# Layer 0's expert jobs packed anew: 42 jobs in place of 43, with the three unranked experts on nine lanes

## The chip, the cores and the metric

The kernel runs on one core of a Trainium2 chip. The metric is device time of one execution in microseconds (us). The core has a matmul engine (PE, with its weight loads as PEld), three engines for element work (DVE, ACT, POOL) and SP, which does no arithmetic: it issues transfers from device memory. POOL issues transfers too, above all those with a list of row numbers (indirect). Each engine takes its instructions in the order in which they stand, so an instruction that waits holds up all that stand behind it on that engine.

## The reference, cut to what matters

Two layers work on 256 latent and 256 context tokens of width 1024. Each layer has a mixer (attention) and then a mixture of experts; in layer 0 both kinds of token pass through the experts, 512 in all:

```python
def moe_ffn(h, w_router, e_bias, w_gate, w_up, w_down, s_gate, s_up, s_down):
    scores = jax.nn.sigmoid((h @ w_router).astype(jnp.float32))
    _, idx = lax.top_k(scores + e_bias.astype(jnp.float32), TOP_K)      # 8 of 64 experts
    wts = jnp.take_along_axis(scores, idx, axis=-1)
    wts = wts / wts.sum(-1, keepdims=True) * ROUTE_SCALE
    ...
    def expert_block(args):
        tok, e = args
        xb = h_pad[tok]
        a = jax.nn.silu(xb @ w_gate[e]) * (xb @ w_up[e])                # 1024 -> 256
        return a @ w_down[e]                                            # 256 -> 1024
    ...
    routed = jnp.zeros((n_tok + 1, d), h.dtype).at[slot_tok].add(y)[:n_tok]
    shared = (jax.nn.silu(h @ s_gate) * (h @ s_up)) @ s_down
    return routed + shared
```

All weights are 32-bit floats, so each of the 64 experts is 3 MB, and every expert is loaded once in each layer.

## The kernel before

**Jobs and lanes.** The experts' work is cut into jobs of 128 slots, one token in a slot. A job has four lanes of 32 slots, and an expert is given as many lanes as it is expected to need. The table is written out by hand in `Plan`: an entry `(column, lane, lanes, offset)` says that an expert's slots from `offset` on lie in these lanes of the job. An expert may be split over two jobs: the same column then stands in both, the second time with the offset at which the first ended. "Column" counts experts in the order in which jobs come to them.

**Unranked and ranked experts.** The first three experts (0, 1 and 2; `ahead` = `NS` = 3) are fixed, so that their weights can be loaded before the router's result is known (`static`). The other 61 are ordered by their number of tokens while the kernel runs (`ranks`); the expert at rank r has as many lanes as the table says, and its number is read from `ordi` before its weights are loaded. In layer 0 before the change, experts 0, 1 and 2 have four lanes each, that is jobs 0, 1 and 2.

**One job.** In the loop over `j`, a job's steps are: `experts` loads the weights of columns not loaded yet (SP; four half-megabyte pieces for gate and up, in two halves `h`, and one megabyte for down); `gate_up` multiplies the 128 slots by gate and up (PE; a job with more than one expert does it lane by lane, several lanes side by side); `act` on ACT and DVE; `gather` fetches the token rows for job j+2 (POOL, indirect; two buffers `xgs` in turn); `slots_T` transposes those of job j+1; `down`; and then the result. A job with one expert after the first three (`passes` 3) splits its weights into two parts and goes through `gate_up3` and `down3`.

**Where results go.** Jobs 3, 5, 7, ... 37 (`sent`) are added to a table in device memory by indirect transfers (`send`, POOL, one for each expert of the job). Every other job is placed by PE (`scatter`: 16 matmuls for a job, spread over the jobs that follow). Near the end `fetch(t)` reads the four token blocks of the two tables back on SP, and DVE adds them to `acc`. The first fetch must wait for the last send; each fetch stands in SP's order at the job in which it is called, behind that job's loads and ahead of the next job's.

**What sets the order.** PE and SP keep the order in which the code is written (`manual_schedule`); the order on DVE, ACT and POOL is a scheduler's. SP can run ahead of PE as far as buffers allow: weights lie in 11 buffers of 1 MB (`w8`), which is under four experts.

**Slots.** `slots` finds, for a group of jobs, which token is in which slot: `marks` on DVE, small matmuls on PE, then `idx`, the list that `gather` uses. The first group has `n0` jobs, those that need no ranking; the second has four, the others `SG` = 8.

Of the kernel before, what the change touches and what calls it, by code (L numbers as in the profile page):

```python
# [39 lines left out]
class Plan:  # L40
# [7 lines left out]
    def __init__(self, layer):  # L48
        self.rank, self.cap, self.jobs = [], [], []
        if layer == 0:  # L50
            self.ahead = 3
            by = {}
            d = self.ahead
            for lanes, n in ((5, 2), (4, 6), (3, 22), (2, 29), (1, 2)):
                by[lanes] = list(range(d, d + n))
                d += n
            for e in range(self.ahead):
                self.single(self.col(e, 4))
            for kind in "ptsptpstp5ptsptpstp5ptsptpstp":
                if kind == "5":  # L60
                    a, b = self.col(by[5].pop(0), 5), self.col(by[3].pop(0), 3)
                    self.single(a)
                    self.jobs.append([(a, 0, 1, 128), (b, 1, 3, 0)])
                elif kind == "s":
                    self.single(self.col(by[4].pop(0), 4))
                elif kind == "t":
                    a, b, c = self.col(by[3].pop(0), 3), self.col(by[3].pop(0), 3), self.col(by[2].pop(0), 2)
                    self.jobs.append([(a, 0, 3, 0), (b, 3, 1, 0)])
                    self.jobs.append([(b, 0, 2, 32), (c, 2, 2, 0)])
                elif by[1]:  # L70
                    self.pack((by[3].pop(0), 3), (by[1].pop(), 1))
                else:
                    self.pair(by[2].pop(0), by[2].pop(0))
        else:
            self.ahead = 4
            self.pair(0, 1)
            self.pair(2, 3)
            two, one = list(range(9, 41)), list(range(41, 64))
            big, three = [4, 5], [6, 7, 8]
            for kind in "ptptspt3ptpt3ptptspt3ptptp":  # L80
                if kind == "s":
                    self.single(self.col(big.pop(0), 4))
                elif kind == "3":
                    self.pack((three.pop(), 3), (one.pop(), 1))
                elif kind == "t":
                    self.pack((two.pop(0), 2), (one.pop(), 1), (one.pop(), 1))
                else:
                    self.pair(two.pop(0), two.pop(0))
        assert sorted(self.rank) == list(range(NE))
# [25 lines left out]
def tile_block(ctx: ExitStack, tc: tile.TileContext, I, out):  # L115
# [25 lines left out]
    def k4(shape, name="k4", dt=F32):  # L141
        return keep.tile(shape, dt, name=name, tag="k4", bufs=NK4)
# [226 lines left out]
    def modrow(l, nm, s):  # L369
        o = MODROW[nm] + (8 * s if nm in ("g1", "B2", "A2", "g2") else 0)  # L370
        return rows(rowsd[l, o:o + 8].rearrange("j p -> (j p)"), 128)
# [662 lines left out]
    def moe(l, out_of, nt, mp, pre=lambda: None, post=lambda: None):  # L1034
        n2 = nt * 128
        pl = PLANS[l]
        NS = pl.ahead
# [30 lines left out]
        def experts(cs):  # L1068
            new = [c for c in cs if c not in have]
            es = [ds(S.value_load(ordi[0:1, c:c + 1], min_val=0, max_val=NE - 1), 1) for c in new]  # L1070
            for c in new:
                have[c] = [[], None]
            for h in range(2):
                for c, e in zip(new, es):
                    have[c][0].extend(load_gu(e, (h,)))
            for c, e in zip(new, es):
                have[c][1] = early.pop(c, None) or expert_dn(c, e)
# [116 lines left out]
        jobs = pl.jobs  # L1194
        njob = len(jobs)
        wsl = mp.tile([128, njob], F32, name="wsl")
        tok = mp.tile([128, njob], F32, name="tok")
        idx = mp.tile([128, njob], I32, name="idx")
# [13 lines left out]
            else:  # L1212
                token_index(i_, t_, sl[:, :, 0])

        n0 = max(j for j in range(njob) if jobs[j][0][0] < NS) + 1
        group = [0, n0, n0 + 4] + list(range(n0 + 4 + SG, njob, SG)) + [njob]

        def all_slots():
# [172 lines left out]
        if l == 0:  # L1391
            xgs = [k4([128, D], f"xg{i}") for i in range(2)]
# [3 lines left out]
        def both(xs, j0, xT):  # L1396
            for k in range(2):
                xs[j0 + k] = lambda j, sl, k=k: xT[j // 4][:, j % 4, k * 128 + sl.start:k * 128 + sl.stop]
# [32 lines left out]
        def gather(x, idx_col):  # L1431
            G.indirect_dma_start(out=x, out_offset=None, in_=h2d[:n2, :],  # L1432
                                 in_offset=bass.IndirectOffsetOnAxis(ap=idx_col, axis=0),
                                 bounds_check=n2 - 1, oob_is_err=False)
# [210 lines left out]
        with tc.manual_schedule(engines={mybir.EngineType.SP, mybir.EngineType.PE}):  # L1645
# [45 lines left out]
            def slots_until(j):  # L1691
                while ready[0] < min(j, njob):
                    next(more)
# [51 lines left out]
            for j in range(njob - l):  # L1745
                segs = jobs[j]
                n_grp = 1 if sent and 2 < j < njob - 4 else GRP
                n_piece = -(-2 * nt // GRP)
                experts([sg_[0] for sg_ in segs])
                if j == njob - 1:  # L1750
                    g2s = [modrow(l, "g2", s) for s in range(nt // 2)]
                    for t in range(nt):
                        xt[t] = k4([128, D], f"xr{t}")
                        S.dma_start(xt[t], xd[t * 128:t * 128 + 128, :])
                ws = [have[sg_[0]] for sg_ in segs]
                if l and j % 2 == 0 and 0 < j < njob - 2:
                    gm = gather_mm(j + 2)
                    both(xs, j + 2, next(gm))
                xT = xs.pop(j)
                if l and j == njob - 2:  # L1760
                    next(gm, None)
                    g2s = [spread(raw[l][:, 5, 0])]
                if j == njob - 1:
                    for _ in sc:
                        pass
                    pre()
                p = pre_p.pop(j, None) or (gate_up3(xT, ws[0]) if passes[j] == 3 else gate_up(xT, ws, segs))
                if l and j == 0:
                    pre_p[1] = gate_up(xs[1], [have[sg_[0]] for sg_ in jobs[1]], jobs[1])
                a = act(p, wsl[:, j:j + 1])  # L1770
                if j == njob - 1:
                    root_table()
                    add[0] = fold(g2s)
                if l:
                    if j == 0:
                        next(rank)
                        sh_step(1)
                        slots_until(3)
                        gm = gather_mm(2)
                        both(xs, 2, next(gm))  # L1780
                        for _ in gm:
                            pass
                        experts((NS, NS + 1))
                        pre_p[2] = gate_up(xs[2], [have[sg_[0]] for sg_ in jobs[2]], jobs[2])
                        sh_step(1, 1)
                    next(gm, None)
                else:
                    if j + 2 < njob:
                        gather(xgs[j % 2], idx[:, j + 2:j + 3])
                    if j + 1 < njob:  # L1790
                        tr = slots_T(xgs[(j + 1) % 2], passes[j + 1])
                        xs[j + 1] = next(tr)
                        next(tr)
                for _ in range(n_piece // 2):
                    next(sc, None)
                aT = act_T(a, passes[j])
                if l == 0:
                    next(tr, None)
                if l == 0 and j == 0:
                    sh_step(3)  # L1800
                for _ in range(n_piece - n_piece // 2):
                    next(sc, None)
                ps = down3(aT, ws[0]) if passes[j] == 3 else down(aT, ws, segs)
                if j == 0:
                    for _ in rank:
                        pass
                next(more, None)
                next(more, None)
                slots_until(j + 1 + LA)
                if j >= n0 + 2:  # L1810
                    next(over, None)
                if l and j == njob - 2:
                    for _ in sc:
                        pass
                    add_x = add[0] = fold(g2s)
                if j in sent:
                    send(j, ps)
                else:
                    grp.append(place(ps, tok[:, j:j + 1]))
                if sent and 0 <= j - (njob - 5) < nt:  # L1820
                    fetch(j - (njob - 5))
                if len(grp) >= n_grp or j >= njob - 2:
                    for _ in sc:
                        pass
                    sc, grp = scatter(grp), []
# [169 lines left out]
```

## Time and profile before

| | us |
|---|---|
| median of three runs (1690.86 to 1693.26) | 1692.18 |
| the profiled execution | 1695.05 |
| its span, from first to last instruction | 1693.3 |
| PE busy in the span | 1572.6 (93%) |
| layer 0's experts, job 0's first matmul to the last job's | about 294 to 929 |

The profiled execution lies 2.9 us above the median, and 1.75 us of it lie outside the span. Times in the rows further down count from the span's start.

### The profile page before, as it was taken

The page shows a single profiled execution, that of the slowest core. Times are in us where ns is not written, and L with a number is a line of the kernel's source. Part 1 is how long each engine was busy: PE and PEld are TensorE (multiplying, and loading weights), DVE is VectorE, ACT ScalarE, POOL GpSimd, SP SyncE. Part 2 cuts the span into 40 slices and gives each one's busy share as a digit, 9 for nine tenths or more (in the row PEclk, how much of TensorE's full clock was granted, in tenths as well). Part 3 has the DMA queues.
Part 4 walks back from the last instruction along what each step waited for, and adds up shares of the span by engine and source line. Part 5 has one row for each costly group of instructions (what it writes and reads, how often), then busy time and mean ns, then how long its engine had stood idle before and what let it go on. Part 6 is the DMA issues. An engine that isn't in the chain of part 4 may idle for free. (4 is left out here: it accounts for less than half of the span.)

```text
span 1693.3 us, 27425 instructions
## 1 busy us (share of the span) xinstructions
PE 1572.6 (93%) x10238; PEld 928.5 (55%) x10238; DVE 784.8 (46%) x2118; ACT 452.0 (27%) x896; POOL 162.9 (10%) x148
## 2 busy tenths in 40 slices
PE   5999999999999999999979799999999998989984
PEld 3765687445445444444434577856656555555542
DVE  2465594356556544435256733347343422223225
ACT  2456311113223223223121333331221211112111
POOL 1003200012111121112200100011000000000001
PEclk9999999999999999999989899999999999999998
DMA  9948866779999999999979855256879999999992
GB/s 328 331 162 299 299 215 212 267 271 371 363 395 341 400 387 398 387 337 389 355 283 408 313 207 199 100 209 262 326 295 420 418 419 419 419 419 419 420 419 107
DMA packets 140808, 549.76 MB, mean 325 GB/s; under 512 B 14288, under 2 KB 23008, under 8 KB 109056
## 3 DMA queue, kind: packets, MB, share of 16 engines
q1 hardware_dynamic: 128368, 510.16, 77.0%
q0 software_dynamic: 12304, 37.81, 7.6%
q8 instruction: 82, 1.34, 0.3%
q14 instruction: 54, 0.44, 0.1%
HBM read 532.63 MB, written 21.05 MB: 327 GB/s over the span
## 5 line engine op out<-in xcount | busy, mean ns | idle before, releaser
L1331 PE MATMUL bank<-w,xT 128*32 128x512 f32 (+2 forms) x1488 | 254.0, 602 | 4.2 <-DMA w<-in_moe_w_up_dram 4.2
L1324 PE MATMUL bank<-w,xT 128*32 128x256 f32 (+2 forms) x2560 | 220.1, 395 | 29.1 <-DMA w<-in_moe_w_up_dram 25.4
L1342 PE MATMUL bank<-w,aT 128*32 128x512 f32 (+2 forms) x1232 | 234.6, 597 | 2.0 <-ACT aT L1298 2.0
L1279 DVE SCALAR_TENSOR_TENSOR a<-s,wsl,bank 128x256 f32<-128x256 f32 x71 | 34.1, 480 | 415.3 <-ACT s L1278 415.3
L1324 PEld LDWEIGHTS bank<-w,xT 128*32 128x32 f32 (+2 forms) x2560 | 130.9, 124 | 116.4 <-DMA w<-in_moe_w_up_dram 33.9
L1521 PE MATMUL bank<-yy,ss 128*128 128x512 f32 x624 | 177.6, 410 | 1.3 <-DVE yy L157 1.0
L1278 ACT ACTIVATE s<-bank 128x256 f32<-128x256 f32 x71 | 27.3, 385 | 544.2 <-PE bank L1331 278.7
L1513 DVE TENSOR_TENSOR acc<-acc,bank 128x512 f32<-128x512 f32 x228 | 149.5, 683 | 45.5 <-PE bank L1521 42.8
L1331 PEld LDWEIGHTS bank<-w,xT 128*32 128x32 f32 (+2 forms) x1488 | 78.6, 125 | 161.0 <-issue 155.0
L1342 PEld LDWEIGHTS bank<-w,aT 128*32 128x32 f32 (+2 forms) x1232 | 67.8, 124 | 120.0 <-issue 106.1
L1521 PEld LDWEIGHTS bank<-yy,ss 128*128 128x128 f32 x624 | 107.4, 190 | 22.5 <-DVE yy L157 2.7
L157 DVE TENSOR_TENSOR yy<-bank,yy 128x512 fp32r<-128x512 f32 x104 | 71.4, 688 | 89.8 <-ACT yy L157 89.8
L157 ACT CAST yy<-bank 128x512 fp32r<-128x512 f32 x104 | 60.9, 586 | 176.6 <-PE bank L1342 158.8
L1432 POOL DMA_INDIRECT xg<-h2d,idx x43 | 51.5, 1198 | 418.4 <-DVE acc L1513 216.8
L157 DVE TENSOR_TENSOR wl<-half,wh 128x1024 fp32r<-128x1024 f32 x35 | 42.7, 1224 | 70.8 <-ACT wh L157 70.8
L1235 DVE TENSOR_SCALAR oh<-ib,pos 128x64 bf16<-128x64 bf16 (+3 forms) x428 | 68.7, 241 | 12.1 <-PE bank L1262 12.0
L161 PE MATMUL bank<-wh,hT 128*128 128x512 f32 x160 | 65.7, 411 | 2.7 <-ACT wh L157 2.1
L162 PE MATMUL bank<-wh,hT 128*128 128x512 f32 x160 | 63.5, 397 | 0.3 <-DVE hT L157 0.2
L163 PE MATMUL bank<-wl,hT 128*128 128x512 f32 x160 | 63.6, 397 | 0.0
L1472 PE MATMUL bank<-ohr,h2p 128*128 128x256 f32 x448 | 60.8, 289 | 0.0
L1472 PEld LDWEIGHTS bank<-ohr,h2p 128*128 128x128 f32 x448 | 55.3, 190 | 8.6 <-PE bank L1324 4.8
L1503 POOL DMA_INDIRECT accd<-yd,idx x32 | 50.2, 1569 | 96.7 <-issue 90.7
(366 smaller groups left out, 2287.7 us busy)
## 6 DMA issues: line engine op xcount, KB each, us to landing
w<-in_moe_w_down_dram SPq DMA_DIRECT2D x104, 1024.0 KB
w<-in_moe_w_gate_dram SPq DMA_DIRECT2D x128, 512.0 KB
w<-in_moe_w_up_dram SPq DMA_DIRECT2D x128, 512.0 KB
w<-in_moe_w_gate_dram SPq DMA_DIRECT2D x64, 1024.0 KB
w<-in_moe_w_up_dram SPq DMA_DIRECT2D x64, 1024.0 KB
w<-in_w_mod_dram SPq DMA_DIRECT2D x24, 1024.0 KB
half<-in_na_w_in_dram SPq DMA_DIRECT2D x12, 1024.0 KB
mh<-in_w_mod_dram SPq DMA_DIRECT2D x12, 1024.0 KB
```

Of the source, the lines that this page charges most:

```text
L157: return A.copy(o_h, src), eng.tensor_sub(o_l, src, o_h.bitcast(F32))
L161: T.matmul(p, xh, wh, start=first, stop=False)
L162: T.matmul(p, xl, wh, start=False, stop=False)
L163: T.matmul(p, xh, wl, start=False, stop=last)
L1235: V.tensor_scalar(oh[:, 32 * lane:32 * (lane + m)], ib[:, off:off + 32 * m], pos[:, t, c:c + 1], None, op0=OP.is_equal)
L1324: T.matmul(p[sl, q * FF:q * FF + FF], xT(j, sl), ws[k][0][q][:, j], start=j == 0, stop=j == NJ - 1, **kw)
L1331: T.matmul(p[sl], xT(j, sl), ws[k][0][j // 4][:, :, j % 4, :], start=j == 0, stop=j == NJ - 1, **kw)
L1342: T.matmul(p[sl], aT[:, j, sl], d[:, n * 512:n * 512 + 512], start=j == 0, stop=j == 1, **kw)
L1432: G.indirect_dma_start(out=x, out_offset=None, in_=h2d[:n2, :], in_offset=bass.IndirectOffsetOnAxis(ap=idx_col, axis=0), bounds_check=n2 - ...
L1472: T.matmul(o, h2p[t][k][:, 2 * q + j], oh[:, t].rearrange("p a b -> p (a b)")[:, :n], start=t == 0 and k == 0, stop=t == nt - 1 and k == 1)
L1513: add = {0: lambda t, r, p: V.tensor_add(acc[t][:, r], acc[t][:, r], p)}
L1521: T.matmul(p, ss[:, t * 128:t * 128 + 128], yy[:, q, r], start=k == 0 and q == 0, stop=k == len(grp) - 1 and q == 1)
```

## The change

The three unranked experts get three lanes each. They no longer fill jobs 0 to 2 alone: job 0 holds expert 0 and one lane of expert 1, job 1 the rest of expert 1 and two lanes of expert 2, job 2 the last lane of expert 2 and, beside it, the first ranked expert with three lanes. One ranked expert (rank 61) goes from two lanes to one, and the last "t" of the table (two jobs for three experts) becomes two pairs. From job 3 to job 39 the same kinds of job stand at the same places, with columns that are one higher; only job 10 is now of three lanes and one, where it was of two and two. With 42 jobs, what is counted from the end stands one job earlier, `fetch` among it. Job 2 now needs the ranking, so `n0` is 2, the slot groups begin one job earlier, and the gather for job 2 moves to a place behind `slots_until`.

```diff
-            for lanes, n in ((5, 2), (4, 6), (3, 22), (2, 29), (1, 2)):
+            for lanes, n in ((5, 2), (4, 6), (3, 22), (2, 28), (1, 3)):
                 by[lanes] = list(range(d, d + n))
                 d += n
             for e in range(self.ahead):
-                self.single(self.col(e, 4))
-            for kind in "ptsptpstp5ptsptpstp5ptsptpstp":
+                self.col(e, 3)
+            a = self.col(by[3].pop(0), 3)
+            self.jobs += [[(0, 0, 3, 0), (1, 3, 1, 0)], [(1, 0, 2, 32), (2, 2, 2, 0)], [(2, 0, 1, 64), (a, 1, 3, 0)]]
+            for kind in "ptsptpstp5ptsptpstp5ptsptpspp":
...
-        n0 = max(j for j in range(njob) if jobs[j][0][0] < NS) + 1
+        n0 = min(j for j in range(njob) if jobs[j][-1][0] >= NS)
...
-                    if j + 2 < njob:
+                    if 0 < j < njob - 2:
                         gather(xgs[j % 2], idx[:, j + 2:j + 3])
...
                 slots_until(j + 1 + LA)
+                if l == j == 0:
+                    gather(xgs[0], idx[:, 2:3])
```

The first place is SP near the end of layer 0's experts. `w` are weights, `ad` is what `fetch` reads from the two tables `accd`, `ordi` and `nbk` are numbers read into registers. Before, from the last weights of job 38 on:

```order
L1054 DMA w_7748<-in_moe_w_down_dram 128x2048
L1510 DMA ad<-accd_77 128x1024
L1510 DMA ad<-accd_78 128x1024
L1070 TENSOR_LOAD ordi
L1070 ISA x2
L1049 ISA
L1049 DMA w_7843<-in_moe_w_gate_dram 128x1024
```

With the change, from the last weights of job 37 on:

```order
L1056 DMA w_7762<-in_moe_w_down_dram 128x2048
L1606 TENSOR_LOAD nbk
L1606 ISA x2
L1512 DMA ad<-accd_77 128x1024
L1512 DMA ad<-accd_78 128x1024
L1072 TENSOR_LOAD ordi
L1072 ISA x2
L1072 TENSOR_LOAD ordi
L1072 ISA x2
L1051 ISA
L1051 DMA w_7861<-in_moe_w_gate_dram 128x1024
```

The last send is that of job 37 in both. Before, the first fetch stood behind the weights of job 38; now it stands ahead of them, and of both its experts.

The second place is POOL at the start of layer 0's experts: `xg` are gathered rows, `accd` the two sends of job 3. Before, from the gather for job 2 on:

```order
L1432 DMA xg_1827<-h2d,idx 128x1024
L1432 DMA xg_1828<-h2d,idx 128x1024
L1432 DMA xg_1827<-h2d,idx 128x1024
L1432 DMA xg_1828<-h2d,idx 128x1024
L1432 DMA xg_1827<-h2d,idx 128x1024
L1503 DMA accd_77<-yd,idx 640x1024
L1503 DMA accd_78<-yd,idx_1826 640x1024
```

With the change, from the same gather on:

```order
L1434 DMA xg_1827<-h2d,idx 128x1024
L1434 DMA xg_1828<-h2d,idx 128x1024
L1434 DMA xg_1827<-h2d,idx 128x1024
L1434 DMA xg_1828<-h2d,idx 128x1024
L1505 DMA accd_77<-yd,idx 640x1024
L1505 DMA accd_78<-yd,idx_1826 640x1024
L1434 DMA xg_1827<-h2d,idx 128x1024
```

The gather for job 6 now stands behind the two sends of job 3. The gather for job 2, the first row, is where it was on POOL, but it now waits for `idx` of the second slot group.

## Rows read from the trace of the kernel before

**Rows 1.** The page, busy time of each engine.
```profile
PE 1572.6 (93%) x10238; PEld 928.5 (55%) x10238; DVE 784.8 (46%) x2118; ACT 452.0 (27%) x896; POOL 162.9 (10%) x148
```
**Rows 2.** Windows: layer 0's experts up to job 37, then jobs 38 to 42.
```profile
core 0: us, PE busy (x) PEld busy (x) DVE busy (x) ACT busy (x) POOL busy (x), PEclk, DMA share, GB/s
294.00:841.00 547.00, 531.09 (x3197) 257.85 (x3197) 275.18 (x729) 147.31 (x256) 93.74 (x69) 0.99 0.96 361
841.00:929.00 88.00, 77.05 (x374) 38.25 (x370) 48.12 (x63) 18.25 (x31) 7.03 (x6) 0.92 0.88 329
```
**Rows 3.** PE's waits, longest first, from 294 to 841.
```profile
PE bank L163 <- DVE wl L157: 5.1, 10, 1.0
```
**Rows 4.** PE's waits, longest first, from 841 to 929.
```profile
PE bank L161 <- ACT wh L157: 5.4, 1, 5.4
PE bank L1331 <- DMA w<-in_moe_w_up_dram: 4.2, 3, 2.6
```
**Rows 5.** Timeline of PE in jobs 38 to 42: start, us, instructions, [idle <-releaser].
```profile
841.13 7.04 PE L1331 MATMUL bank<-w,xT 128*64 128x512 f32 x32
...
860.29 0.80 PE L161 MATMUL bank<-wh,xT 128*128 128x512 f32 x1 [5.42 <-ACT wh L157]
...
877.42 1.06 PE L1331 MATMUL bank<-w,xT 128*32 128x512 f32 x6 [1.45 <-DMA w<-in_moe_w_up_dram]
881.10 9.46 PE L1331 MATMUL bank<-w,xT 128*32 128x512 f32 x58 [2.62 <-DMA w<-in_moe_w_up_dram]
...
905.60 0.66 PE L1446 MATMUL bank<-head,xg 128*128 128x128 f32 x4
...
914.13 7.57 PE L1521 MATMUL bank<-yy,ss 128*128 128x512 f32 x32
921.63 7.09 PE L1331 MATMUL bank<-w,xT 128*64 128x512 f32 x32
```
**Rows 6.** Timeline of SP's queue, from job 38's last weights to job 40's first.
```profile
827.88 3.66 SPq L1054 DMA_DIRECT2D w<-in_moe_w_down_dram  x2
847.51 2.38 SPq L1510 DMA_DIRECT2D ad<-accd  x2
850.73 0.34 SPq L1049 DMA_DIRECT2D w<-in_moe_w_gate_dram  x1
...
868.73 0.81 SPq L1510 DMA_DIRECT2D ad<-accd  x2
870.90 0.35 SPq L1049 DMA_DIRECT2D w<-in_moe_w_gate_dram  x1
```
**Rows 7.** Timeline of POOL: job 37's first send, and the gather for job 42.
```profile
842.81 1.47 POOL L1503 DMA_INDIRECT accd<-yd,idx  x1 [4.72 <-issue]
...
871.02 1.94 POOL L1432 DMA_INDIRECT xg<-h2d,idx  x1 [19.34 <-DVE acc L1513]
```
**Rows 8.** Timeline of ACT: the first cast of job 39's weights.
```profile
859.19 1.99 ACT L157 CAST wh<-w 128x1024 fp32r<-128x1024 f32 x2 [3.69 <-DMA w<-in_moe_w_up_dram]
```
**Rows 9.** Windows of 5 us behind the two stalls; columns as in Rows 2.
```profile
860.00:865.00 5.00, 4.67 (x10) 3.28 (x11) 4.50 (x4) 3.17 (x4) 0.00 (x0) 0.50 0.55 232
...
880.00:885.00 5.00, 3.90 (x20) 1.12 (x24) 0.00 (x0) 0.00 (x0) 0.00 (x0) 0.50 1.04 403
```
**Rows 10.** Timeline of PE: first and last gate/up matmul of job 34 (24).
```profile
787.15 0.50 PE L161 MATMUL bank<-wh,xT 128*128 128x512 f32 x1
...
792.52 0.39 PE L163 MATMUL bank<-wl,xT 128*128 128x512 f32 x1
```
**Rows 11.** Timeline of PE: gate/up of job 0, transposes in job 1.
```profile
294.53 7.03 PE L1331 MATMUL bank<-w,xT 128*128 128x512 f32 x16
...
321.30 0.60 PE L1446 MATMUL bank<-head,xg 128*128 128x128 f32 x4
```
**Rows 12.** Timeline of DVE: marks of slots in job 0.
```profile
294.99 2.43 DVE L1235 TENSOR_SCALAR oh<-ib,pos 128x96 bf16<-128x96 bf16 x16
...
310.71 1.91 DVE L1235 TENSOR_SCALAR oh<-ib,pos 128x64 bf16<-128x64 bf16 x12 [0.71 <-PE bank L1262]
```
**Rows 13.** Timeline of POOL: the gather for job 3.
```profile
315.07 0.99 POOL L1432 DMA_INDIRECT xg<-h2d,idx  x1 [19.57 <-issue]
```

## The prediction

> **What bounds the kernel now.** The page comes first: PE is busy for 93% of the span [rows 1], but a share over the whole span says nothing of a single stage. So the windows come next, cut at layer 0's experts. From job 0 to the end of job 37 PE is busy for 531 of 547 us, and transfers run at 361 GB/s with a share of 0.96; in jobs 38 to 42 both fall, to 77 of 88 us and to 329 GB/s [rows 2]. The waits tell why. In the long stretch PE's costliest wait is 5.1 us in ten pieces, on DVE, and no transfer is in its list ahead of that [rows 3]: PE is the bound there, with weights always there in time. In the last five jobs it waits for weights, 5.4 us through a cast and 4.2 us directly [rows 4].
>
> The timelines show where these waits come from. SP has job 38's last weights out by 831.5 and then does nothing until 847.51: there stands the first fetch, and it waits for job 37's send, which POOL issues at 842.81 [rows 6, 7]. Job 39's weights stand behind it and leave at 850.73 [rows 6]; ACT can cast them from 859.19 and PE starts at 860.29 after 5.42 us idle [rows 5, 8]. The same happens again one job later: the second fetch leaves at 868.73, after job 39's gate/up, whose buffers it needs; job 40's weights follow at 870.90, and PE runs fully only from 881.10 [rows 5, 6]. After both stalls the granted clock is 0.50, the lower of the two levels (1.2 of 2.4 GHz) [rows 9]. A stage bound by PE gains from a job less; the last five jobs are bound by SP's order.
>
> **What the job less is worth.** Job 38 takes 13.7 us (841.13 to 860.29, less the 5.42) [rows 5]. If nothing else changed, the end would come some 14 us earlier.
>
> **Start: +0.6 us.** Job 0's gate/up takes 7.03 us as 16 matmuls over the whole array, and a job of lanes 7.04 or 7.09 [rows 5, 11], so lanes cost nothing per job. The Trainium skill (TensorEngine Tiling (Array Packing), Key Properties) says that a change of tiling mode drains the engine, which speaks against three more jobs in lanes; it gives no price. These rows bound it at 0.06 us a job, so 0.2 us at most in the sum; I take nothing. In job 0 DVE now marks slots of jobs 2 to 5 in the second group: behind the first 16 marks come 16 small ones where 12 stood. Sixteen took 2.43 us, the twelve 1.91 [rows 12]: +0.5, and PE's small matmuls behind them wait as long; I add 0.3 for the buffers that they share, and take off 0.2 for the four matmuls that the first group loses. The gather for job 2 needs that group's list, as job 3's did at 315.07 [rows 13], so it leaves at about 316. Job 1's transposes need it; they stood at 321.30 [rows 11] and come at about 322. No row shows how long a gather takes to land; the nearest is the send, issued at 842.81, for which the fetch at 847.51 had waited: 4.7 us [rows 6, 7]. That makes 320.7, 1.3 us in hand. Bounds: -0.2 if the marks hide, +3 if the gather takes half as long again. The gather for job 6 goes behind two sends, some 10 us later, but its transposes are more than 20 us away: nothing.
>
> **Jobs 3 to 37: nothing.** The weights of a job wait for buffers that PE gives back, and from job 5 on the same kinds of job hand back the same buffers at the same places. Job 2's extra expert loads from 290 on, when two buffers lie unused, and has 35 us. So job 37 ends where it did, at 841.1 plus the start.
>
> **The end, step by step.** The first fetch now stands ahead of job 38's weights, both experts of them; before, those had long landed. In the clock of the old trace:
>
> 1. The fetch leaves at 847.5 as before, since it waits for the same send; the weights leave 3.2 us later [rows 6], and 0.5 more for a second number to be read (1.36 us from the end of the second fetch to 870.90, against 0.84): 851.2.
> 2. From the first of two experts' weights to PE at full work took 10.2 us (870.90 to 881.10) [rows 5, 6]. A gather of half a megabyte ran at the same time (871.02) [rows 7], 1.3 us at 403 GB/s [rows 9], and has no partner here: 8.9 us, so 860.1. Bounds: 8.5 us, what one expert took (850.73 to 859.19) [rows 6, 8], and 10.2. PE stands still for 19.0 us.
> 3. The clock is low afterwards: 58 of 64 matmuls took 9.46 us where 7.04 is the price of 64 [rows 5], so +3.0.
> 4. Job 38 ends at 860.1 + 3.0 + 13.7 = 876.8.
> 5. Job 39's weights now follow without a wait. Behind job 38's first halves lie 4.2 MB of its others, 1.05 MB of the second fetch, 0.5 MB of a gather and 1.05 MB of job 39's own first half: 6.8 MB at 403 GB/s are 16.9 us, 877.0, and the first cast takes 1.1 us [rows 5, 8]: 878.1, 1.3 us idle. Its gate/up takes 5.8 us as in job 34 (787.15 to 792.91) [rows 10], not the 8.4 of before (860.29 to 868.73) [rows 5, 6], as after so short a pause I leave the clock high: 883.9.
> 6. The third fetch waits for just that, as the second did. From 868.73 to 881.10 were 12.4 us; less the gather, 11.1: job 40 runs from 895.0, and its gate/up ends at 904.5, low clock included. Job 39's rest (7.2 us before, less without scatter) hides in this wait.
> 7. Job 40's rest is as long as that of job 41 before, 8.5 us (905.60 to 914.13), and the scatter ahead of the last gate/up takes 7.5 again [rows 5]: the last gate/up starts at 920.5, where it stood at 921.63 [rows 5]. Its two experts' weights are 10.5 MB behind the third fetch, 26 us at 403 GB/s: 910 and some us to land, in time.
>
> So the last gate/up, and the end with it, comes 1.1 us earlier (920.5 against 921.63): nearly all of the job less goes into the stall of 19.0 us and the low clock behind it. With the start the sum is -0.5 us: 1694.5 for the profiled execution, 1691.7 against the median, which lies 2.9 lower. Bounds: -1.6 by steps 1 and 2, +2 (gather), +2.7 (clock in job 39).
>
> The Trainium skill (DMA: Bandwidth & Descriptors, Anatomy of one DMA) says that transfer engines do not wait on semaphores; the issuing sequencer does, before it dispatches. By that, all behind the fetch on SP is held, weights that wait for nothing too. The trace agrees: nothing left SP between 831.5 and 847.51 [rows 6].
>
> **Rivals.**
> - *The forecast: the stall at job 38 eats the job.* 1691.7. Chance 0.57.
> - *The stall does not come, or is half as long,* because the queue lies idle ahead of it and sends and weights land sooner. For: the 4.7 us of the send ran beside the last weights. Against: a single expert took 8.5 us with as idle a queue. With no stall 1678; with 12 us in place of 19, some 7 us less, 1685. Faster begins where the stall is under 16 us. Chance 0.22.
> - *Slower: transfers do not run at 403 GB/s behind the stall.* The end then hangs on bytes, in a row from step 2 to the last job. At the 329 GB/s of the stretch [rows 2] step 5's 16.9 us become 20.7 (+3.8) and step 6's two experts take 1.3 more: 1696.8. It decides from about 340 GB/s down, or with the low clock in job 39 from 370. For: such a queue has gaps. Against: 403 in the row behind the second stall [rows 9]. Chance 0.21.
> - *The change does not do what it says:* an expert with more tokens than slots runs extra blocks. By the reference's routing of its own inputs, experts 0, 1 and 2 have 73, 47 and 37 tokens for 96 slots and rank 61 has 31 for 32. No block; chance nil.
>
> **Numbers.** A measurement tells about 0.2% (3.4 us) from no change. Within it falls the forecast, 0.57; faster 0.22, slower 0.21. The range reaches from the halved stall, 1685, to the slower rival with some of the bounds of the start, 1699.
>
> **What would show it.** Right: SP's first `ad` near 847.5 with no weights between job 37's and it; PE idle some 19 us before job 38, then a clock of 0.50; a small pause before job 39, one of 5 to 6 us in job 40; the last gate/up within 2 us of 921. Wrong: job 38's weights ahead of the fetch, or PE idle under 12 us there; waits for `xg` in job 1; PE waiting for weights in jobs 3 to 37, which would say that buffers do not come back as before; or a later layer that does not simply shift.

## The result and the profile after

The changed kernel takes 1702.67 us (median of five runs, 1702.12 to 1709.63), the kernel before 1692.18: a ratio of 1.0071, with a 95% interval from 1.0056 to 1.0087. It is slower by 10 to 12 us; the forecast was 1691.7 and no change. The profiled execution of the changed kernel is the median one, with a span of 1700.8 us.

The windows first, cut as in [rows 2], with the same columns:

```profile
294.00:841.00 547.00, 529.68 (x3386) 251.93 (x3380) 272.93 (x719) 144.95 (x252) 92.91 (x69) 0.99 0.95 354
841.00:929.00 88.00, 59.25 (x226) 30.87 (x222) 34.80 (x44) 15.58 (x25) 5.10 (x5) 0.83 0.86 316
```

The long stretch looks as before. In the last one PE is busy for 59 of 88 us where it was busy for 77, and the waits of PE from 841 to 929 say for what it stands still:

```profile
PE bank L1333 <- DMA w<-in_moe_w_up_dram: 24.3, 5, 18.2
PE bank L163 <- ACT wh L159: 2.1, 1, 2.1
```

Weights, in five pieces, one of 18.2 us. The timeline of SP shows the order behind it (`ad` is what a fetch reads):

```profile
849.03 2.74 SPq L1512 DMA_DIRECT2D ad<-accd  x2
853.20 0.34 SPq L1051 DMA_DIRECT2D w<-in_moe_w_gate_dram  x1
...
862.02 1.99 SPq L1512 DMA_DIRECT2D ad<-accd  x2
865.15 0.34 SPq L1051 DMA_DIRECT2D w<-in_moe_w_gate_dram  x1
...
889.69 0.81 SPq L1512 DMA_DIRECT2D ad<-accd  x2
891.87 0.34 SPq L1051 DMA_DIRECT2D w<-in_moe_w_gate_dram  x1
```

The first fetch leaves 6.5 us behind the place where job 38 would start without a pause (842.53, worked out below), and before it was 6.4 (847.51 [rows 6] less 841.13 [rows 5]). But now job 38's weights stand behind it and leave at 853.20. And the timeline of PE in jobs 38 to 41:

```profile
860.87 1.94 PE L1333 MATMUL bank<-w,xT 128*64 128x512 f32 x2 [18.17 <-DMA w<-in_moe_w_up_dram]
863.73 5.01 PE L1333 MATMUL bank<-w,xT 128*64 128x512 f32 x16 [0.92 <-DMA w<-in_moe_w_up_dram]
869.10 3.62 PE L1333 MATMUL bank<-w,xT 128*64 128x512 f32 x14 [0.36 <-DMA w<-in_moe_w_up_dram]
...
881.48 0.50 PE L163 MATMUL bank<-wh,xT 128*128 128x512 f32 x1 [2.06 <-ACT wh L159]
...
882.74 0.50 PE L165 MATMUL bank<-wl,xT 128*128 128x512 f32 x1 [0.52 <-DVE wl L159]
...
884.78 0.63 PE L165 MATMUL bank<-wl,xT 128*128 128x512 f32 x1
...
889.26 0.39 PE L165 MATMUL bank<-wl,xT 128*128 128x512 f32 x1
...
897.79 1.04 PE L1333 MATMUL bank<-w,xT 128*64 128x512 f32 x2
900.73 5.80 PE L1333 MATMUL bank<-w,xT 128*64 128x512 f32 x16 [1.90 <-DMA w<-in_moe_w_up_dram]
909.47 3.62 PE L1333 MATMUL bank<-w,xT 128*64 128x512 f32 x14 [2.94 <-DMA w<-in_moe_w_up_dram]
...
929.05 7.09 PE L1333 MATMUL bank<-w,xT 128*64 128x512 f32 x32
```

The pause ahead of job 38 is 18.17 us, and the last gate/up starts at 929.05 where it stood at 921.63 [rows 5]: 7.4 us later, though a job is gone. All that follows simply shifts: the spans differ by 7.5 us.

The medians differ by 10.5, and the other 3 us hide in the kernel before: its profiled execution was 2.9 us above its median. Job 0's gate/up started at 294.53 there [rows 11], at 292.91 after the change, and at 292.86 and 292.96 in two experiments below that have the old packing. What comes ahead of job 0 thus varies from one execution to the next, so stages are counted from job 0 in what follows. From there to the place where job 38 would start without a pause (842.53: 828.92 and a job of 13.61) the change takes 549.6 us. The kernel before takes 546.6 in its profile and 545.0 in the run of 43 jobs with POOL's fetches below: 3.0 to 4.6 us are lost where the prediction had 0.6. Most of what lies between those two is job 1, and there it is the clock. Job 1's gate/up after the change, and in the kernel before:

```profile
311.92 7.09 PE L1333 MATMUL bank<-w,xT 128*64 128x512 f32 x32
```

```profile
312.77 8.69 PE L1331 MATMUL bank<-w,xT 128*128 128x512 f32 x16
```

From 314 to 316 the granted clock is 1.00 in the first and 0.51 in the second. So the changed kernel is best held against the 545.0, where job 1's gate/up took 7.10 us.

The place of the loss is job 3. PE's timeline of its end and of job 4:

```profile
356.38 0.36 PE L1264 MATMUL bank<-wt,oh 128*128 128x15 bf16 x8
357.24 1.55 PE L1264 MATMUL bank<-wt,oh 128*128 128x15 bf16 x7 [0.49 <-DVE oh L1237]
...
360.38 8.77 PE L1333 MATMUL bank<-w,xT 128*32 128x512 f32 x64
```

and DVE's beside it:

```profile
356.93 3.68 DVE L1237 TENSOR_SCALAR oh<-ib,pos 128x128 bf16<-128x128 bf16 x23
```

Job 3 takes 19.73 us from gate/up to gate/up (340.65 to 360.38). 23 marks of slots stand in one piece on DVE, PE's small matmuls follow at DVE's pace, and job 4's gate/up then takes 8.77 us, where a job of lanes takes 7.04 or 7.09 [rows 5]: the granted clock is 0.50 from 362 to 364.

### The profile page after: what moved, and what is told of

Read it like the earlier page. It is cut to its first block, busy times and chain, and to the rows that moved or that the text cites. A ratio compares the mean times of both kernels' runs of the same rounds, so it can differ in the third digit from the quotient of the medians.

```text
span 1700.8 us, 27576 instructions
## 1 busy us (share of the span) xinstructions
PE 1559.7 (92%) x10328; PEld 916.1 (54%) x10328; DVE 778.5 (46%) x2110; ACT 449.2 (26%) x890; POOL 160.1 (9%) x147
## 5 line engine op out<-in xcount | busy, mean ns | idle before, releaser
L1333 PE MATMUL bank<-w,xT 128*32 128x512 f32 (+1 forms) x1568 | 249.2, 604 | 24.4 <-DMA w<-in_moe_w_up_dram 24.3
L1326 PEld LDWEIGHTS bank<-w,xT 128*32 128x32 f32 (+2 forms) x2560 | 129.8, 124 | 117.8 <-DMA w<-in_moe_w_up_dram 32.9
L1523 PE MATMUL bank<-yy,ss 128*128 128x512 f32 x608 | 172.9, 410 | 1.3 <-DVE yy L159 1.0
L1333 PEld LDWEIGHTS bank<-w,xT 128*32 128x32 f32 (+1 forms) x1568 | 73.8, 122 | 181.5 <-issue 171.9
L1515 DVE TENSOR_TENSOR acc<-acc,bank 128x512 f32<-128x512 f32 x220 | 144.1, 682 | 46.1 <-PE bank L1523 43.8
L1344 PEld LDWEIGHTS bank<-w,aT 128*32 128x32 f32 (+2 forms) x1240 | 67.9, 123 | 117.5 <-issue 103.9
```

What stands on the lines that cost most here:

```text
L1326: T.matmul(p[sl, q * FF:q * FF + FF], xT(j, sl), ws[k][0][q][:, j], start=j == 0, stop=j == NJ - 1, **kw)
L1333: T.matmul(p[sl], xT(j, sl), ws[k][0][j // 4][:, :, j % 4, :], start=j == 0, stop=j == NJ - 1, **kw)
L1344: T.matmul(p[sl], aT[:, j, sl], d[:, n * 512:n * 512 + 512], start=j == 0, stop=j == 1, **kw)
L1515: add = {0: lambda t, r, p: V.tensor_add(acc[t][:, r], acc[t][:, r], p)}
L1523: T.matmul(p, ss[:, t * 128:t * 128 + 128], yy[:, q, r], start=k == 0 and q == 0, stop=k == len(grp) - 1 and q == 1)
```

## The experiments

Each changes the kernel named in its expectation; times are medians, ratios stand against runs of the kernel before on the same chip.

**The fetches one job later.**

```diff
-                if sent and 0 <= j - (njob - 5) < nt:
-                    fetch(j - (njob - 5))
+                if sent and 0 <= j - (njob - 4) < nt:
+                    fetch(j - (njob - 4))
```

> The changed kernel, with the four fetches called in jobs 38 to 41 as before the change, so that job 38's weights stand ahead of the first fetch again. Theory (SP's order is the whole loss): job 38 follows job 37 without a pause at about 842.7 in the clock of the changed kernel's trace, the end looks as before the change but is one job shorter: the last gate/up starts near 908 where it stood at 929.05, and the time is 1682 us (1679 to 1688), some 20 below the changed kernel and 10 below the kernel before. Rival (the new packing itself, or transfers that are slow whatever the order, make the loss): the stall only moves to another job, and the time stays within 5 us of 1702.7.

1688.44 us, ratio 0.9975 (0.9964 to 0.9987): 14 below the changed kernel, 5 below the one before. PE's timeline:

```profile
843.04 7.04 PE L1333 MATMUL bank<-w,xT 128*64 128x512 f32 x32
...
862.38 0.79 PE L163 MATMUL bank<-wh,xT 128*128 128x512 f32 x1 [5.60 <-ACT wh L159]
...
910.96 7.09 PE L1333 MATMUL bank<-w,xT 128*64 128x512 f32 x32
```

The pause at job 38 is gone, and the old one of 5.6 us at job 39 is back. From job 38 to the last gate/up it takes 67.9 us (910.96 less 843.04), before the change 80.5 (921.63 less 841.13 [rows 5]): the job less is worth 12.6 there, near the forecast 14. But the time shows only 5, so a loss lies elsewhere too.

**The early fetch alone, with 43 jobs** (`njob - 6` in the same lines of the kernel before).

> The kernel before, with 43 jobs, and only the four fetches called one job earlier (37 to 40). Theory: the stall of 18 us comes at job 38 with the old packing too, and two low-clock jobs behind it; the time is 1710 us (1704 to 1714), 12 to 22 above the kernel before. Rival (the packing makes the loss): within 4 us of 1692.2.

1711.80, ratio 1.0116 (1.0098 to 1.0135). PE's timeline:

```profile
856.98 1.94 PE L1331 MATMUL bank<-w,xT 128*64 128x512 f32 x2 [17.31 <-DMA w<-in_moe_w_up_dram]
```

The pause comes with the old packing as well. Its whole price, with all that follows it, is 18.4 us (1711.80 less 1693.41); less the 5 that the packing gives without it, that makes 13.4, against the 10.5 measured of the whole change. The two intervals, some 3 us to either side, cover that difference.

**POOL issues the fetches**, with 42 jobs and with 43:

```diff
-                S.dma_start(y, a[t * 128:t * 128 + 128, :])
+                G.dma_start(y, a[t * 128:t * 128 + 128, :])
```

> The changed kernel, with the eight table transfers issued by POOL, so that SP's weights wait for no send. Theory: no pause at job 38 and none of 2 us and more in jobs 39 and 40 that is for weights; the clock stays at its upper level; the time is 1670 us (1664 to 1680), some 33 below the changed kernel. Rival (what is left to transfer bounds the end, in whatever order): pauses of the same sum at jobs 40 and 41, and no more than 20 below the changed kernel, as with the fetches one job later.

> The kernel before, 43 jobs, with the eight table transfers issued by POOL. Theory: the pauses of 5.42, 1.45 and 2.62 us and the low clock behind them go, some 12 us: 1680 us (1675 to 1686). The difference to the changed kernel with the same edit is what one job less is worth when nothing on SP waits: 13.7 by the theory, under 8 if the packing has a price of its own.

1681.76 (0.9932) and 1685.00 (0.9954), 3.2 us apart. SP is free, but with 42 jobs PE does not run on. Its timeline in job 38:

```profile
866.84 0.70 PE L1296 MATMUL bank<-head,a 128*128 128x128 f32 x2 [13.17 <-DVE a L1281]
```

and DVE's:

```profile
861.99 1.23 DVE L1513 TENSOR_TENSOR acc<-acc,ad 128x1024 f32<-128x1024 f32 x1 [15.94 <-DMA ad<-accd]
```

DVE holds the add of the table ahead of job 38's activation, so the wait for the send has only moved from SP to DVE: 13.2 us with 42 jobs, more than the 12 by which 1670 was missed. I had not thought of it. With 43 jobs it is 6.7 us, in job 39's gate/up:

```profile
860.82 0.80 PE L163 MATMUL bank<-wl,xT 128*128 128x512 f32 x1 [6.72 <-DVE wl L157]
```

As the two waits differ, the 3.2 us between the runs are not the worth of a job.

**The last send two jobs earlier** (`range(3, njob - 6, 2)` for `sent`).

> The changed kernel with the fetches where it has them, but job 37 placed by PE, so that the last send is job 35's, some 27 us earlier. If it is the wait for the send that holds SP (and not the fetch's place or its 4 MB as such): the first fetch leaves near 835 without a wait, the pause of 18 us at job 38 goes, PE places one job more (7.5 us), and the second fetch still waits for the buffers of job 39's gate/up: 1692 us (1688 to 1696). If the place and the bytes of the fetch make the pause, a pause of over 12 us stays at job 38 and the time is 1700 or more.

1680.79, ratio 0.9925 (0.9906 to 0.9945). The second of the two transfers of SP's first fetch (the first left at 825.55), and job 38 on PE:

```profile
827.70 0.33 SPq L1512 DMA_DIRECT2D ad<-accd  x1
```

```profile
845.51 7.09 PE L1333 MATMUL bank<-w,xT 128*64 128x512 f32 x32
```

The fetch stands in the same place and moves the same bytes, and there is no pause: it is the wait for job 37's send that holds the weights, not place or bytes. The expected 1692 was 11 too high; job 37 took 15.77 us in place of 13.61, so placing it cost 2.2 us and not 7.5, which is about half of that.

**The old edges of the slot groups**, on top of the first experiment:

```diff
-        group = [0, n0, n0 + 4] + list(range(n0 + 4 + SG, njob, SG)) + [njob]
+        group = [0, n0, 7] + list(range(7 + SG, njob, SG)) + [njob]
```

> The 42 jobs with the fetches one job later, as in the first experiment, and the edges of the slot groups at 7, 15, 23, 31, 39 as before the change in place of 6, 14, 22, 30, 38 (the second group then has five jobs). The changed kernel's jobs 0 to 37 take 3.0 us longer than before the change, of which job 3 alone 3.9: there the rest of the third group's marks is due, one job earlier than before. Theory (the groups' due time): job 3 takes 15.9 us again in place of 19.8, job 0 some 0.8 more, and the time is 3 us below the first experiment's: 1685 (1683 to 1688). Rival (the added ranked expert in job 2 or its gather makes the loss): job 3 stays near 19.8, and the time within 1 us of 1688.4.

1684.39, ratio 0.9952 (0.9937 to 0.9967): 4.1 below the first experiment. PE's timeline from job 3 to job 4, and DVE's marks beside it:

```profile
343.37 7.07 PE L1333 MATMUL bank<-w,xT 128*32 128x512 f32 x64
...
359.19 7.07 PE L1333 MATMUL bank<-w,xT 128*32 128x512 f32 x64
```

```profile
359.66 2.43 DVE L1237 TENSOR_SCALAR oh<-ib,pos 128x96 bf16<-128x96 bf16 x16
```

Job 3 takes 15.8 us again, and job 38 starts 546.7 us behind job 0 (841.47 less 294.73), 2.9 earlier than the 549.6 of the changed kernel. The loss in job 3 was the groups' due time, not the ranked expert in job 2. Against the 545.0 of the old packing, 1.7 us remain: job 0, where the second group now has five jobs, takes 19.5 us in place of 18.2.

**Fetches behind the weights, in a buffer of their own**, with 42 jobs, and with 43. The core of it (with 43 jobs the last two fetches have a job each):

```diff
-                y = k4([128, D], "ad")
+            y = t8([128, 2, D], "ad", F32)
...
                 experts([sg_[0] for sg_ in segs])
+                if sent:
+                    for t in {njob - 3: [0], njob - 2: [1], njob - 1: [2, 3]}.get(j, ()):
+                        fetch(t)
```

> The 42 jobs, each fetch behind the weights of the job in which it stands (first fetch behind job 39's weights, second behind job 40's, the last two behind job 41's), and with a buffer that does not wait for job 39's gate/up. Theory (SP's order is what the last jobs wait for): no wait of PE for weights over 1 us in jobs 38 to 40, the clock stays at its upper level there, jobs 38 to 41 run at 13 to 15 us each, and the time is 1675 us (1671 to 1682), some 13 below the first experiment's. Rival (bytes bound the end): pauses at jobs 40 and 41, and the time within 4 us of 1688.

> The kernel before, 43 jobs, with the same edit: fetches behind the weights of jobs 39, 40, 41 and 42. Against the run with 42 jobs and this edit it gives the worth of one job when SP's order holds nothing. Prediction's step (a job is worth 13.7 us), less the 3 us that the packing costs in jobs 0 to 37: 10.7 apart, 1685 us (1681 to 1690). Rival (the end of the layer is bound by bytes, which a job less does not change): the two are within 4 us.

1684.91 (0.9952) and 1683.16 (0.9947): the same. No weights are waited for any more; the last gate/up with 42 jobs stands at 900.45, 10.5 us earlier than in the first experiment, and yet the time is within 4 us of it. PE's timeline at the border to the next layer, where L271 and L287 are the first matmuls for it:

```profile
920.22 3.64 PE L271 MATMUL bank<-half,scT 128*32 128x512 f32 x32
...
933.58 1.12 PE L287 MATMUL bank<-head,mods 128*128 128x128 f32 x4 [9.13 <-ACT mods L293]
```

With 43 jobs the same two follow each other from 929.00 on without a wait, but just ahead of them PE waits for DVE:

```profile
924.25 4.81 PE L1521 MATMUL bank<-yy,ss 128*128 128x512 f32 x13 [4.34 <-DVE yy L157]
```

With 42 jobs the wait is put down to ACT, whose copy stands behind a step for which DVE must have folded tables and sums into the rows; and DVE adds two pairs of tables behind the last gate/up, the first and the last of four adds here (with 43 jobs it is one pair):

```profile
908.48 1.22 DVE L1513 TENSOR_TENSOR acc<-acc,ad 128x1024 f32<-128x1024 f32 x1
...
916.61 1.22 DVE L1513 TENSOR_TENSOR acc<-acc,ad 128x1024 f32<-128x1024 f32 x1
```

So it was not bytes that bound the end, as the rivals had it; their numbers came true through DVE.

**Both repairs and early sends**, with 42 jobs (old group edges, last send in job 35, fetches behind the weights of jobs 38 to 41) and with 43.

> 42 jobs with three repairs together: last send in job 35, each fetch behind the weights of jobs 38 to 41 with a buffer of its own, slot groups with the edges of before the change. Theory (the job less is given back by SP's waits, by the groups' due time and, with the tables late, by DVE at the layer's end): no wait of PE for weights over 1 us in jobs 38 to 41, and DVE adds only one table pair after the last gate/up: 1672 us (1667 to 1678), 7 to 9 below the best so far. Rival (another bound stands at the border to the next layer, near 1681, as three quite different versions came out at 1681 to 1685): 1680 or more.

> The kernel before, 43 jobs, with last send in job 35 and the fetches behind the weights of jobs 38 to 41 with the same buffer. Its slot groups had the good edges already, so against the run with 42 jobs this is the worth of one job alone. Prediction's step: 13.7 us apart. Theory as it stands now (what follows the layer also hangs on DVE's work behind the last job, which is the same in both): 9 to 13.7 apart, 1683 us (1680 to 1688). Rival (border to the next layer): under 4 apart.

1677.05, ratio 0.9894 (0.9875 to 0.9914), and 1682.22, 0.9932 (0.9919 to 0.9946): 5.2 apart. PE at the border with 42 jobs, and with 43:

```profile
916.85 3.64 PE L271 MATMUL bank<-half,scT 128*32 128x512 f32 x32
...
927.77 1.11 PE L287 MATMUL bank<-head,mods 128*128 128x128 f32 x4 [6.69 <-ACT mods L293]
```

```profile
933.60 3.64 PE L269 MATMUL bank<-half,scT 128*32 128x512 f32 x32
...
938.66 0.66 PE L285 MATMUL bank<-head,mods 128*128 128x128 f32 x4 [0.83 <-ACT mods L291]
```

Counted from job 0 (294.20 and 296.55), PE comes to the next layer's first matmul 14.4 us earlier with 42 jobs, about the worth of a job; then it waits 6.7 us there, and 0.8 with 43. The 14.4 are a balance: job 39's gate/up took 12.4 us with 43 jobs, where it waited 3.6 for DVE, and 9.0 with 42, while jobs 0 to 2 took 2.9 us longer with 42.

**Sends as in the change, one pair less for the last job** (old edges, fetches behind job 39, job 40 twice, job 41).

> 42 jobs with the old slot groups, sends to job 37 as in the changed kernel, fetches behind the weights of jobs 39 (first), 40 (second and third) and 41 (fourth). It differs from the seventh experiment in the groups and in that one table pair, not two, is left for the last job. If DVE's adds behind the last job were what took that experiment's gain: 1677 us (1673 to 1681), 8 below it, of which 3 to 4 are the groups. If not: 1681 or more, the groups alone.

1679.23, ratio 0.9909 (0.9893 to 0.9924): 5.7 below the version with two pairs, of which 4 are the edges. It waits 6.7 us at the border in place of 9.1. The time lies in the expected range; the 1.6 us that are left for the table pair are less than the runs' spread.

**Fetches behind the weights of jobs 37 to 40**, otherwise as two experiments ago.

> The 42 jobs with last send in job 35 and the old slot groups, the fetches behind the weights of jobs 37 to 40 instead of 38 to 41, so that no table is added behind the last gate/up, as with 43 jobs. In the version before it PE came to the next layer 14.4 us earlier than with 43 jobs (both counted from job 0), but 6 us of that were lost again in a wait for DVE. If DVE's adds behind the last gate/up are that wait: the wait of 6.7 us shrinks to 1 or 2 us, 1672 us (1669 to 1675), 10 or more below the 43 jobs' 1682.2, near the 13.7 of the prediction's step. If another bound stands at the border: 1676 to 1679, no gain.

1674.01, ratio 0.9889 (0.9867 to 0.9912): the lowest time, but on another chip, and by its ratio not told apart from the 0.9894 of two experiments ago. PE at the border:

```profile
920.30 3.64 PE L271 MATMUL bank<-half,scT 128*32 128x512 f32 x32
...
926.63 0.66 PE L287 MATMUL bank<-head,mods 128*128 128x128 f32 x4 [2.10 <-ACT mods L293]
```

The wait is 2.1 us in place of 6.7, and from the last gate/up to the second of these matmuls it takes 24.1 us (902.58 to 926.63) in place of 28.7 (899.12 to 927.77), so the wait was for DVE's table adds. That the time gains by it is not shown: in this profile PE comes to the border 3.3 us later, counted from job 0, as the gate/ups of jobs 1 and 25 ran in part at a clock of 0.50. Against 43 jobs it is 8.2 us by the medians and 7 by the ratios; the 10 that I expected are not reached.

**PE kept busy in the pause.** Matmuls on constants, unread, ahead of job 38's gate/up of the changed kernel; first 46, then 23:

```diff
+                if l == 0 and j == njob - 4:
+                    warm_p = bank()
+                    for k in range(46):
+                        T.matmul(warm_p[:, :384], ident, head[:, :384], start=k == 0, stop=k == 45)
```

> The changed kernel with 46 matmuls of 384 columns on constants ahead of job 38's gate/up, whose result nobody reads, in the pause of 18 us: the weights come when they came, but PE does not stand still. If the low clock behind the pause has a price of its own (prediction: 3.0 us in job 38, and the clock high in job 39): clock at its upper level in job 38 and its gate/up 1 to 3 us shorter, job 39's start nearly unchanged as it waits for weights, its gate/up 5.8 to 6.4 in place of 8.2, and the time 2 to 5 us lower, 1698 to 1701. If the weights alone set the end: within 1.5 us of 1702.7.

> The changed kernel with 23 matmuls on constants in the pause at job 38; each takes two passes, 0.65 us, as the run with 46 showed (30 us, 15 longer than the pause left room for), so PE works 15 us and is free before the weights come at 860 to 869. If the low clock behind the pause has a price: granted clock at its upper level when job 38 starts, its gate/up 10 to 11 us in place of 11.85, the pause of 2.06 us ahead of job 39 and the low clock in it unchanged (with 46 matmuls job 39 showed it too), and the time 1 to 2 us below the changed kernel, 1700 to 1703. If job 39's low clock came from job 38's: its gate/up 5.8 to 6.4 us and 1697 to 1700.

1710.81 (1.0093) and 1705.98 (1.0084, 1.0060 to 1.0107). The first tells little of job 38: its matmuls were two records each, 29.94 us, and job 38 started at 876.08, behind its weights. The second ends in time. PE's timeline:

```profile
845.44 15.10 PE L1772 MATMUL bank<-head 128*128 128x384 f32 x46
863.27 1.04 PE L1333 MATMUL bank<-w,xT 128*64 128x512 f32 x2 [2.72 <-DMA w<-in_moe_w_up_dram]
866.25 5.10 PE L1333 MATMUL bank<-w,xT 128*64 128x512 f32 x16 [1.94 <-DMA w<-in_moe_w_up_dram]
872.32 3.62 PE L1333 MATMUL bank<-w,xT 128*64 128x512 f32 x14 [0.97 <-DMA w<-in_moe_w_up_dram]
```

and its window where job 38 begins:

```profile
860.00:865.00 5.00, 1.58 (x4) 0.19 (x2) 0.05 (x1) 0.00 (x0) 0.00 (x0) 1.00 1.02 371
865.00:870.00 5.00, 3.75 (x12) 1.38 (x14) 0.00 (x0) 0.00 (x0) 0.00 (x0) 0.66 1.00 344
```

The clock is 1.00 where the gate/up begins, and was 0.50 in the changed kernel. But behind the wait of 1.94 us it falls inside the gate/up, to 0.50 from 866 to 868, and 16 matmuls take 5.10 us there, as in the changed kernel (5.01). So the run kept the clock high only for the first two matmuls, and its weights left SP 1.2 us later behind the start of the pause than the changed kernel's (857.32 less 845.44, against 853.20 less 842.53). It does not give the price of the low clock by itself. The gate/up takes 12.7 us (863.27 to 875.94) against 11.85; inside it PE waits 2.9 us for weights, where it waited 1.3. In both runs the last 14 matmuls start when their weights have landed (waits of 0.97 and 0.36 us) and take 3.62 us. The interval of the time, 1.0060 to 1.0107, covers the changed kernel's 1.0071, so no gain is seen. Job 39 shows eight slow matmuls of 0.59 to 0.63 us in the run with 46 too, where job 38's gate/up had run in one piece of 7.09 us.

## Why the prediction was wrong

**Right: the mechanism and its first step.** The fetch ahead of two experts' weights, held by the send, stops PE for 18.2 us where 19.0 were forecast, and the pause's price is shown twice: put into the old kernel it costs 18.4 us, and without the wait for the send it is gone. The lanes cost nothing (7.04 to 7.09 us a gate/up), the gather for job 2 came in time (no idle ahead of job 1's transposes), job 0 took 0.8 us more (19.01 against 18.24), forecast 0.6. The later layer shifts.

**Failed: "Jobs 3 to 37: nothing."** That part counted weights and buffers, but not the slot groups that it had itself seen begin one job earlier. Job j asks for the slots of all jobs up to j + 3 (`slots_until(j + 1 + LA)`). With an edge at 7 the third group is due in job 4, with the edge at 6 in job 3, and its eight jobs, two steps of which are made in each job from job 1 on, have one job less in which to be spread; what is left comes in one piece. Against the old packing where job 1 took 13.0 us, as in the changed kernel (12.9), the stretch lost 4.6 us (549.6 less 545.0), forecast 0.6: 4.0 of the miss. The run with the old edges takes 2.9 of the 4.6 back in its profile, and 4.1 us in time.

**Mis-sized: what follows the pause.** From the place where job 38 would have started to the last gate/up the steps made 79.4 us (841.1 to 920.5), measured are 86.5 (842.53 to 929.05): 7.1 too few, of which the pause itself gives back 0.8.
- Step 3 had 10.0 us for job 38's gate/up, with 3.0 for the low clock. It took 11.85 (+1.8). The low clock is in it (1.94 us for the first two matmuls, 1.04 in the run with 23 matmuls on constants), but it does not set the end: the last 14 matmuls wait 0.36 us for their weights, so a faster clock ahead of them would only have made that wait longer. The weights still arrive during the gate/up; step 2 had priced PE "at full work" by a row of job 40, where 58 of 64 matmuls then ran in one piece.
- Step 5 had 1.3 us of pause and a gate/up of 5.8 us in job 39. It was 2.06 (+0.8) and 8.17 (881.48 to 889.65, +2.4). Here the clock is most of the reason: eight matmuls of 0.59 to 0.63 us, against 0.39 at the end of the same gate/up. In the run with the earlier last send, where the clock stayed high in it, the same gate/up took 6.58 us, with the same wait of 0.5 for DVE inside it: 1.6 of the 2.4 are the clock, 0.8 that wait. The forecast left the clock high after so short a pause, and that choice failed; the row of job 39 itself, 8.4 us [rows 5, 6], was at hand. Thirteen of the 16 profiles show 7 to 14 such slow matmuls in job 39; the three without have the early fetch with 43 jobs, POOL's fetches with 42 and the earlier last send.
- Step 6 had 20.6 us from the third fetch to the end of job 40's gate/up (883.9 to 904.5); it took 23.4 (889.69 to 913.1), with a second wait of 2.94 us for the second halves, which had followed without a wait in [rows 5], in a job of narrower lanes: +2.8.
- Step 7 held: 16.0 us forecast from there to the last gate/up, 16.0 measured.

Together 4.0 + 7.1 = 11.1; the miss is 11.0 (1702.67 less 1691.7). That they meet so well is partly the choice of the 545.0: the four traces of the old packing up to there lie between 543.4 and 546.6, and with those the sum would be 12.7 or 9.5.

**The rivals.** The one on the slower side gave 1696.8 through slow transfers. Two windows of 5 us behind the pause:

```profile
858.00:863.00 5.00, 1.94 (x2) 0.29 (x2) 0.00 (x0) 0.00 (x0) 0.00 (x0) 0.50 0.98 339
868.00:873.00 5.00, 4.64 (x21) 1.55 (x18) 0.00 (x0) 0.19 (x1) 0.00 (x0) 1.00 1.01 419
```

From the leaving of job 38's first weights to the cast of job 39's it took 27.2 us (853.20 to 880.38), 25.8 were reckoned to their landing. Slow transfers are a small part, and that side came true for other reasons. The rival of a halved stall failed: from the leaving of the first weights to PE it took 7.7 us (853.20 to 860.87) where 8.9 were reckoned, so the idle queue saved 1.2 us at most.

**What one job is worth.** The 13.7 us nearly hold on PE (14.4 and 12.6 in two pairs of runs, each with other differences in it), but the time shows it only so far as nothing else at the layer's end waits: SP's fetches, DVE's adds of what they bring, and DVE's work at the border. The best version with 42 jobs is 1.1% below the kernel before (ratio 0.9889), and nearly the same repairs without the job less gave 0.7% (0.9932): 7 us. The traces show pieces of what is missing: with 42 jobs and the old edges job 0 takes 1.2 us more and job 2 0.3, the wait at the border is 1.3 us longer, and job 1's gate/up ran at the lower clock in three of four profiles, for 1.3 to 2.9 us. These are single executions, so for the medians it stays open; the executions of each version spread over 5 to 8 us.

## What to carry to other kernels

When a count sets a loop's length, list everything that is placed by counting from its end or from its start, and price each of them moved past what it now stands ahead of: here two such rules, the fetches and the slot groups, cost more than the work saved. A transfer that waits should stand behind all that does not wait, and so should the instruction that consumes it: moved to another queue, the wait reappeared on DVE. And behind a long pause, reckon the jobs that follow by the worst row that the trace has of them, not the best.

## What the runs showed of the hardware

- Behind pauses of 1.63 and 0.53 us, job 39's gate/up had eight matmuls of 0.59 to 0.63 us in the run with 46 matmuls on constants, and none in the run with the earlier last send. What tells the two apart no run shows.
- With PE busy for 15 us of the pause, job 38's gate/up began at a clock of 1.00 in place of 0.50, but the clock fell to 0.50 inside it, behind a wait of 1.94 us for weights.
- Job 0 started between 292.7 and 296.6 us into the span in 16 profiles, which no edit explains.
- Job 1's gate/up took 7.1 us where the clock stayed at 1.00, 8.4 to 8.8 where it was 0.50 for part of it, and 9.9 to 10.0 where that part was longer, also between profiles whose code is the same up to there. Behind what the clock fell in one and not in the other no run shows. Whoever compares two profiles should first take such stretches out.
- A matmul of 32-bit floats with constants of 384 columns stood in the trace as two records of together 0.65 us.
